# Two additions of the fast down projection moved between its items, and a longer planned wait ahead of the cross-chunk products of a recurrence

## The chip, the cores and the metric

The kernel runs on one core of one Trainium2 chip. The metric is the device time of one execution in microseconds (us), lower is better. A core has a matrix engine (PE, with its weight loads shown as a row of their own, PEld), a vector engine (DVE), a scalar engine (ACT), GpSimd (POOL) and SyncE (SP), which here only issues transfers. Each engine works through its own list of instructions in the order in which they were put there, and an instruction that waits for another engine holds up what stands behind it on its own.

## The reference

Two decoder layers on x of 512 tokens by 1024 channels, everything in float32. Each layer is a half-weighted SwiGLU block, a mixer and a second half-weighted SwiGLU block, each between two RMS norms:

```python
x = x + 0.5 * rms_norm(swiglu(rms_norm(x, g0), w_gate1, w_up1, w_down1), g1)      # 1024 -> 2816 -> 1024
h = rms_norm(x, g2); hq, hf, hi, hg, aq, ak, av, gate_a, gate_b = split(h @ w_in)
A = hgrn2_mixer(hq, hf, hi, hg, ...) @ w_branch_hgrn     # gated linear recurrence, 4 heads, 128 x 128
B = swa_sink_attention(aq, ak, av, sinks) @ w_branch_attn # window 128, 8 query and 2 key heads
x = x + rms_norm((sigmoid(gate_a) * A + sigmoid(gate_b) * B) @ w_out, g3)
x = x + 0.5 * rms_norm(swiglu(rms_norm(x, g4), w_gate2, w_up2, w_down2), g5)
```

In the recurrence a head's state is decayed by a gate per channel and token and takes up an outer product of key and value; the output is the state read with the query. The kernel computes it without a scan, as a causal 512 x 512 matrix of decayed scores times the values.

## The kernel before

**Products.** A float32 factor is carried as two parts, `hi` (rounded to the matrix engine's fast format) and `lo` (what is left), and a product is three matmuls, hi·hi, hi·lo and lo·hi (`mm3`). Every weight tile is loaded from DRAM by SP into one of four buffers `w32` (in the profile `w`), then ACT copies it into `whi` (L281 for the items of the fast down projection, L324 for the others) and DVE subtracts that from the tile into `wlo` (L286, L331). There are six `whi` and six `wlo` buffers, so the split runs a few items ahead of PE. A buffer of `w32` comes free, and the next load is issued, when the last split that reads it is done.

**The fast down projection.** Four times, once in each SwiGLU block, eight of the 22 blocks of rows of the down projection's weights (8 x 8 blocks of 128 x 128) are multiplied by a scheme of seven instead of eight products of quarters (`ORDER`: p1, p6, p2, p7, p5, p4, p3). Each product is 24 matmuls of 512 columns, from two items with q = 0 and 1, and `quarters` writes their order for PE. `quarter` prepares an item: p1, p2, p4 and p5 use a raw quarter of the weights, the others sums of quarters. With b12 and b22 loaded beside the raw tiles, p6 makes `t2` = b11 - b12 - b22 in a buffer of the tag `tt` (L267, L268). p7 adds b22 onto b12 (L276), which is its own weight, and also adds t2 onto the raw quarter b21 (L277), which only p4 reads. Each addition is two instructions of 128 x 512 per item. `pin` keeps the additions of these lines in the written order among themselves. On DVE there also stand the sums of the products' results: `add` (L789) forms u2 from product 6 and p1, u3 from product 7 and u2, and later two more from product 5. L789 reads PSUM and so waits for the product's matmuls, and the PSUM buffer of the product comes free when it is done.

The tag `tt` has two buffers. The tile `grow` (a row of gains, L664) is the next to take the older one, so its transfer, issued by SP, waits for the last reader of t2.

**The order of PE.** PE's order is written out while the program is built: the main line of the program issues projections and products, and after each it polls a planner (`Order`), which keeps a planned time `t` in ns and adds to it a price for every matmul. Work that depends on other engines is written as generators. Each yields a number of planned ns (the table `WAIT`), and its next piece is put into PE's order at the first poll at which that many planned ns have passed, with a pause of WAIT["rest"] between two pieces. For the other engines a scheduler chooses the order from the program's text and its own estimates, so that it moves when PE's order moves.

**The recurrence.** `recurrence_scores` handles two heads at a time, twice per layer. Its last steps are:

```python
yield WAIT["last"]            # then p1 = aux(): products of chunks 0,1 and 2,3 of both heads
...                           # L1047, L1048: eight scalings of the keys and queries, in place, on DVE; L1049 copies p1
yield WAIT["chunks"]
for h in hs:                  # the cross-chunk products of the two heads, one PSUM buffer each
    h.s2 = big(F32, [P, 2, 2 * P]); p2 = aux()
    for s in range(2):
        mm(p2[:, s * 256 : (s + 1) * 256], h.kz[:, s * P : (s + 1) * P], h.qa[:, 256:512], True, True)
    nc.scalar.copy(h.s2, p2...)   # L1057
```

PSUM buffers of the tag `aux` (three of them) serve these products, the scores of the attention (`attend`, two buffers at a time, read by DVE at L1157) and others in turn. A softmax block of the attention continues on ACT (L1174) and returns to DVE (L1178: `den`). The first pair of heads runs while PE computes the values of the recurrence from the tokens (`project_tok`, four `acc` buffers), beside the attention's first blocks; the second pair while PE computes the branches.

Of the kernel before, what the change touches and what calls it, by code (L numbers as in the profile page):

```python
# [11 lines left out]
ALU = mybir.AluOpType  # L12
# [18 lines left out]

WAIT = dict(
    first=0.0, spread=2300.0, squares=1700.0, lay=34500.0, laid=770.0, normed=7600.0, final=2600.0,
    head=2600.0, level=5000.0, last=3400.0, chunks=1270.0, blocks=350.0, norm=2370.0, gate=8000.0,
    values=1200.0, scores=2000.0, exp=9000.0, shares=4500.0, turn=1900.0, turned=3000.0, rest=1200.0, lent=4200.0, apart=4000.0, block=2000.0, pair=4000.0, att0=1260.0, att1=12300.0,
)
W32, WS, AHEAD, TAIL, PLAIN, FIRST, EARLY, LATE = 4, 6, 3, 4, 4, 7, 4, 8
# [8 lines left out]
def trunk(ctx: ExitStack, tc: tile.TileContext, xin, wall, gains, lbT, hgain, sinks, c_dist, c_mask, c_ident, out):  # L46
    nc = tc.nc
# [11 lines left out]
    def nm(s):  # L59
        seq[0] += 1  # L60
        return f"{s}_{seq[0]}"
# [83 lines left out]
    pin = tc.keep_in_program_order  # L145
# [10 lines left out]
    class Stream:  # L156
# [98 lines left out]
        def quarter(self, it):  # L255

            self.load(it.base + 4)
            q, h = it.q, (slice(0, S), slice(S, D))
            if it.kind in ("p1", "p2", "p5", "p4"):
                w = [self.raw[it.u][:, c] for c in h]  # L260
            elif it.kind == "p6":

                t = sb.tile([P, D], F32, tag="tt", name=nm("tt"), bufs=2)
                self.t2[q] = w = [t[:, c] for c in h]
                for c in range(2):
                    t1 = self.raw[it.u][:, h[c]]
                    pin(nc.vector.tensor_tensor(t1, t1, self.b12[q][c], op=ALU.subtract))  # L267
                    pin(nc.vector.tensor_tensor(w[c], t1, self.b22[q][c], op=ALU.subtract))  # L268
            elif it.kind == "p3":
                w = self.b22[q]  # L270
            elif it.kind == "p7":

                w = self.b12[q]
                for c in range(2):
                    b21 = self.raw[it.base + 2 + q][:, h[c]]
                    pin(nc.vector.tensor_tensor(w[c], w[c], self.b22[q][c], op=ALU.add))  # L276
                    pin(nc.vector.tensor_tensor(b21, b21, self.t2[q][c], op=ALU.add))  # L277
            it.hi = sb.tile([P, D], F32R, tag="whi", name=nm("whi"), bufs=WS)
            it.lo = sb.tile([P, D], F32R, tag="wlo", name=nm("wlo"), bufs=WS)
            for c in range(2):  # L280
                nc.scalar.copy(it.hi[:, h[c]], w[c])  # L281
                if it.kind in DMAS:
                    nc.scalar.mul(it.lo[:, h[c]], w[c], -1.0)
                    nc.gpsimd.dma_start(it.lo[:, h[c]].bitcast(F32), w[c], accum_op=ALU.add)
                else:
                    nc.vector.tensor_tensor(it.lo[:, h[c]], w[c], it.hi[:, h[c]].bitcast(F32), op=ALU.subtract)  # L286
            self.done += 1
            self.flight += 1
            if it.kind in ("p5", "p4"):
                self.raw.pop(it.u)  # L290
                self.freed += 1
                self.load(self.freed + W32)
# [1158 lines left out]
```

## Time and profile before

| | |
|---|---|
| median of 3 runs | 2108.14 us (2106.92 to 2108.67) |
| the profiled execution | 2106.95 us, span in the trace 2104.9 us, so 2.05 us lie around the span |
| its place among the runs | 1.19 us below the median |
| granted clock of PE | 0.999 |
| busy PE, PEld, DVE, ACT, POOL | 2093.2, 1875.4, 1549.3, 1122.6, 154.2 us |

The page gives each engine's busy time and share of the span. The view of waits sums, by the line that waited and the line that ended the wait, how long an engine stood idle. The timeline lists instructions by their start, equal neighbours merged: start, duration, engine, line, operation, tiles, shapes, count, and in brackets the idle time ahead of it and what ended it. Matmuls overlap, so the spacing of their starts says how fast they go, and not their durations.

### The profile page before, as it was taken

The page shows a single profiled execution, that of the slowest core. Times are in us where ns is not written, and L with a number is a line of the kernel's source. Part 1 is how long each engine was busy: PE and PEld are TensorE (multiplying, and loading weights), DVE is VectorE, ACT ScalarE, POOL GpSimd, SP SyncE. Part 2 cuts the span into 40 slices and gives each one's busy share as a digit, 9 for nine tenths or more (in the row PEclk, how much of TensorE's full clock was granted, in tenths as well). Part 3 has the DMA queues.
Part 4 walks back from the last instruction along what each step waited for, and adds up shares of the span by engine and source line. Part 5 has one row for each costly group of instructions (what it writes and reads, how often), then busy time and mean ns, then how long its engine had stood idle before and what let it go on. Part 6 is the DMA issues. An engine that isn't in the chain of part 4 may idle for free.

```text
span 2104.9 us, 35214 instructions
## 1 busy us (share of the span) xinstructions
PE 2093.2 (99%) x13549; PEld 1875.4 (89%) x13549; DVE 1549.3 (74%) x2705; ACT 1122.6 (53%) x1899; POOL 154.2 (7%) x188
## 2 busy tenths in 40 slices
PE   9999999999999999999999999999999999999998
PEld 7899988877888999998899998898778989999987
DVE  5877886766776777789587778767686758777884
ACT  6555554446454555556355556444654545555562
POOL 0011000000000011110001110000000000111000
PEclk9999999999999999999999999999999999999999
DMA  8677653312236357774447775632122563677651
GB/s 247 152 181 184 176 164 127 111 61 70 72 101 201 127 123 181 181 194 128 151 114 176 183 181 149 190 121 91 51 81 61 136 190 106 158 182 181 182 164 47
DMA packets 148071, 298.35 MB, mean 142 GB/s; under 512 B 16992, under 2 KB 74816, under 8 KB 147904
## 3 DMA queue, kind: packets, MB, share of 16 engines
q1 hardware_dynamic: 122416, 228.16, 33.1%
q0 software_dynamic: 25344, 67.91, 18.7%
q8 instruction: 106, 1.74, 0.3%
q14 instruction: 61, 0.50, 0.1%
q10 hardware_dynamic: 144, 0.05, 0.0%
HBM read 213.43 MB, written 14.73 MB: 108 GB/s over the span
## 4 chain that ended last, share of the span: by engine, by line
PE 80%; DVE 9%; ACT 6%; issue 2%; DMA 2%; SPq 0%; ACTq 0%; DVEq 0%
PE acc L115 59%; PE aux L115 19%; ACT whi L324 2%; DMA w<-wall 2%; DVE s L401 1%; PE aux L125 1%; DVE wlo L331 1%; DVE wlo L286 1%; ACT s L400 1%; ACT m L894 1%; ACT wlo L328 1%; PE acc L125 1%; DVE tt L318 1%; DVE tt L311 1%; DVE tt L268 0%
## 5 line engine op out<-in xcount | busy, mean ns | idle before, releaser
L115 PE MATMUL acc<-s,whi 128*128 128x256 f32 (+1 forms) x4952 | 1059.4, 311 | 0.9 <-ACT whi L324 0.7
L115 PEld LDWEIGHTS acc<-s,whi 128*128 128x128 f32 x4952 | 808.0, 191 | 51.8 <-issue 3.2
L115 PE MATMUL acc<-s,wlo 128*128 128x256 f32 (+1 forms) x2476 | 766.6, 310 | 0.1
L115 PEld LDWEIGHTS acc<-s,wlo 128*128 128x128 f32 x2476 | 472.6, 191 | 25.2 <-DVE wlo L331 0.4
L324 ACT CAST whi<-w 128x1024 fp32r<-128x1024 f32 (+1 forms) x341 | 317.0, 948 | 259.2 <-PE acc L115 99.9
L115 PE MATMUL acc<-whi,s 128*128 128x512 f32 x1264 | 414.0, 393 | 0.0
L324 ACT CAST whi<-tt 128x1024 fp32r<-128x1024 f32 x154 | 161.4, 1048 | 326.6 <-DVE tt L318 182.8
L331 DVE TENSOR_TENSOR wlo<-w,whi 128x1024 fp32r<-128x1024 f32 (+1 forms) x181 | 218.1, 1215 | 156.5 <-ACT whi L324 149.4
L115 PEld LDWEIGHTS acc<-whi,s 128*128 128x128 f32 x1264 | 237.1, 188 | 54.9 <-ACT whi L324 1.6
L331 DVE TENSOR_TENSOR wlo<-tt,whi 128x1024 fp32r<-128x1024 f32 x154 | 188.0, 1221 | 97.4 <-ACT whi L324 97.3
L115 PE MATMUL acc<-wlo,s 128*128 128x512 f32 x632 | 246.9, 391 | 1.0 <-DVE wlo L286 1.0
L115 PE MATMUL aux<-s,whi 128*128 128x256 f32 (+1 forms) x1248 | 230.5, 285 | 0.0
L329 POOL DMA_DIRECT2D wlo<-w x160 | 137.8, 863 | 1259.6 <-ACT wlo L328 732.2
L115 PE MATMUL aux<-whi,s 128*128 128x512 f32 x592 | 196.8, 390 | 0.0
L115 PEld LDWEIGHTS aux<-s,whi 128*128 128x128 f32 x1248 | 195.2, 192 | 1.1 <-issue 0.5
L115 PE MATMUL aux<-s,wlo 128*128 128x256 f32 (+1 forms) x624 | 177.6, 285 | 0.0
L115 PEld LDWEIGHTS acc<-wlo,s 128*128 128x128 f32 x632 | 118.7, 188 | 25.6 <-DVE wlo L286 2.4
L115 PEld LDWEIGHTS aux<-whi,s 128*128 128x128 f32 x592 | 111.1, 188 | 22.9
L328 ACT ACTIVATE wlo<-w 128x1024 fp32r<-128x1024 f32 (+1 forms) x160 | 129.8, 844 | 0.0
L400 ACT CAST s<-s 128x512 fp32r<-128x512 f32 (+1 forms) x164 | 88.6, 580 | 70.7 <-DVE s L459 66.6
L115 PEld LDWEIGHTS aux<-s,wlo 128*128 128x128 f32 x624 | 119.8, 192 | 0.4
L115 PE MATMUL aux<-wlo,s 128*128 128x512 f32 x296 | 115.2, 389 | 0.0
(186 smaller groups left out, 2127.6 us busy)
## 6 DMA issues: line engine op xcount, KB each, us to landing
w<-wall SPq DMA_DIRECT2D x267, 512.0 KB, 3.7
wlo<-w POOLq DMA_DIRECT2D x83, 512.0 KB, 5.5
w<-wall SPq DMA_DIRECT2D x288, 128.0 KB, 3.2
wlo<-w POOLq DMA_DIRECT2D x77, 256.0 KB, 3.3
x_d<-s SPq DMA_DIRECT2D x48, 256.0 KB, 2.1
s<-x_d SPq DMA_DIRECT2D x48, 256.0 KB, 5.3
w<-wall SPq DMA_DIRECT2D x34, 256.0 KB, 3.0
s<-wall SPq DMA_DIRECT2D x64, 128.0 KB, 3.6
```

Of the source, the lines that this page charges most:

```text
L115: nc.tensor.matmul(o, lhsT, rhs, start=start, stop=stop)
L125: nc.tensor.transpose(o, src, ident)
L286: nc.vector.tensor_tensor(it.lo[:, h[c]], w[c], it.hi[:, h[c]].bitcast(F32), op=ALU.subtract)
L311: pin(nc.vector.tensor_tensor(self.t13[:, h[0]], w[:, h[0]], v[:, h[0]], op=ALU.add))
L318: pin(nc.vector.tensor_tensor(t[:, h[1]], t[:, h[0]], w[:, h[1]], op=ALU.add))
L324: i = nc.scalar.copy(it.hi[:, c], w[:, c])
L328: nc.scalar.mul(it.lo[:, c], w[:, c], -1.0)
L329: nc.gpsimd.dma_start(it.lo[:, c].bitcast(F32), w[:, c], accum_op=ALU.add)
L331: nc.vector.tensor_tensor(it.lo[:, c], w[:, c], it.hi[:, c].bitcast(F32), op=ALU.subtract)
L400: nc.scalar.copy(hi, src)
L401: nc.vector.tensor_tensor(lo, src, hi.bitcast(F32), op=ALU.subtract)
L894: nc.scalar.activation(out=m[:, 0:2, :], in_=m[:, 0:2, :], func=AF.Silu)
```

## The change

Two edits. The two additions of t2 onto b21 leave item p7 and stand at the head of item p4 with the same q. The planned wait `chunks`, between the products of neighbouring chunks and the cross-chunk products, goes from 1270 to 2600 planned ns. The number of instructions is the same on every engine.

```diff
-    head=2600.0, level=5000.0, last=3400.0, chunks=1270.0, blocks=350.0, norm=2370.0, gate=8000.0,
+    head=2600.0, level=5000.0, last=3400.0, chunks=2600.0, blocks=350.0, norm=2370.0, gate=8000.0,
...
             if it.kind in ("p1", "p2", "p5", "p4"):
                 w = [self.raw[it.u][:, c] for c in h]
+                if it.kind == "p4":
+                    for c in range(2):
+                        pin(nc.vector.tensor_tensor(w[c], w[c], self.t2[q][c], op=ALU.add))
...
                 w = self.b12[q]
                 for c in range(2):
-                    b21 = self.raw[it.base + 2 + q][:, h[c]]
                     pin(nc.vector.tensor_tensor(w[c], w[c], self.b22[q][c], op=ALU.add))
-                    pin(nc.vector.tensor_tensor(b21, b21, self.t2[q][c], op=ALU.add))
```

The changed lines shift the later lines of the file. Inside `quarter`, L276 of before is L278 now and the moved additions are L263; from L278 of before on a line is one higher (L286 is L287, L664 is L665, L789 is L790, L1057 is L1058, L1157 is L1158).

The first place is DVE in the first of the four fast down projections, where the items of p7 are made; w_489 and w_492 are the raw b21 of q = 0 and 1, s_2765 to s_2772 are b12, s_2777 to s_2784 b22, s_3131 and s_3132 the two halves of u2. Before:

```order
L276 TENSOR_TENSOR s_2765<-s_2765,s_2777 128x512
L277 TENSOR_TENSOR w_489_2817<-w_489_2817,tt_2996 128x512
L276 TENSOR_TENSOR s_2766<-s_2766,s_2778 128x512
L277 TENSOR_TENSOR w_489_2817<-w_489_2817,tt_2996 128x512
L286 TENSOR_TENSOR wlo_3166<-s_2765,whi_3165 128x512
L286 TENSOR_TENSOR wlo_3166<-s_2766,whi_3165 128x512
L276 TENSOR_TENSOR s_2771<-s_2771,s_2783 128x512
L277 TENSOR_TENSOR w_492_2840<-w_492_2840,tt_3044 128x512
L276 TENSOR_TENSOR s_2772<-s_2772,s_2784 128x512
L277 TENSOR_TENSOR w_492_2840<-w_492_2840,tt_3044 128x512
L286 TENSOR_TENSOR wlo_3179<-s_2771,whi_3178 128x512
L286 TENSOR_TENSOR wlo_3179<-s_2772,whi_3178 128x512
```

These twelve are followed by the two additions to u2 (L789). Now, from behind the first two additions of L278 on:

```order
L790 TENSOR_TENSOR s_3131<-aux_3159,s_3129 128x512
L287 TENSOR_TENSOR wlo_3164<-s_2765,whi_3163 128x512
L287 TENSOR_TENSOR wlo_3164<-s_2766,whi_3163 128x512
L278 TENSOR_TENSOR s_2771<-s_2771,s_2783 128x512
L278 TENSOR_TENSOR s_2772<-s_2772,s_2784 128x512
L790 TENSOR_TENSOR s_3132<-aux_3160,s_3130 128x512
L287 TENSOR_TENSOR wlo_3175<-s_2771,whi_3174 128x512
L287 TENSOR_TENSOR wlo_3175<-s_2772,whi_3174 128x512
L287 TENSOR_TENSOR wlo_3204<-w_467_2710,whi_3203 128x512 x2
L287 TENSOR_TENSOR wlo_3218<-w_478_2760,whi_3217 128x512 x2
L263 TENSOR_TENSOR w_489_2817<-w_489_2817,tt_2996 128x512 x2
L790 TENSOR_TENSOR s_3133<-acc_3249,s_3131 128x512
```

Both halves of u2 have moved ahead of p7's `wlo`, one to each item, the additions onto b21 stand behind p5's `wlo`, and the first half of u3 (s_3133, from product 7) now stands ahead of p4's `wlo`.

The second place is PE in the mixer of the first layer, at the first pair of heads; acc_4617 to acc_4620 are the values projected from the tokens, aux_4766 and aux_4771 (now aux_4804 and aux_4809) the cross-chunk products of the two heads, aux_4788 and aux_4789 (now aux_4775 and aux_4776) the first scores of the attention's next block. Before:

```order
L115 MATMUL acc_4620<-whi_4486,s_3867 128x512
L115 MATMUL acc_4620<-wlo_4487,s_3867 128x512
L115 MATMUL acc_4620<-whi_4486,s_3868 128x512
L115 MATMUL aux_4766<-s_4258,s_4220 128x256 x2
L115 MATMUL aux_4771<-s_4263,s_4230 128x256 x2
L115 MATMUL acc_4617<-whi_4486,s_3870 128x512
L115 MATMUL acc_4617<-wlo_4487,s_3870 128x512
L115 MATMUL acc_4617<-whi_4486,s_3871 128x512
L115 MATMUL acc_4618<-whi_4486,s_3870 128x512
L115 MATMUL acc_4618<-wlo_4487,s_3870 128x512
L115 MATMUL acc_4618<-whi_4486,s_3871 128x512
L115 MATMUL aux_4788<-s_4290,s_4378 128x256
```

Now, three matmuls of acc_4617 and the twelve of the scores stand ahead of these:

```order
L115 MATMUL aux_4776<-s_4290,s_4424 128x256
L115 MATMUL acc_4618<-whi_4486,s_3870 128x512
L115 MATMUL acc_4618<-wlo_4487,s_3870 128x512
L115 MATMUL acc_4618<-whi_4486,s_3871 128x512
L115 MATMUL acc_4619<-whi_4486,s_3870 128x512
L115 MATMUL acc_4619<-wlo_4487,s_3870 128x512
L115 MATMUL acc_4619<-whi_4486,s_3871 128x512
L115 MATMUL aux_4804<-s_4258,s_4220 128x256 x2
L115 MATMUL aux_4809<-s_4263,s_4230 128x256 x2
L115 MATMUL acc_4620<-whi_4486,s_3870 128x512
```

The cross-chunk products have moved behind nine matmuls of the values and the twelve of the first scores, so these scores now take their PSUM buffers first. DVE follows: the readings of these scores (L1157) now stand ahead of `den` (L1178), behind which they stood.

At the second pair of heads of a layer the cross-chunk products move behind nine matmuls of a branch, and the outputs of these two heads with them. On SP, in each fast down projection, the transfer of `grow` now stands behind the eight transfers of the next two weight tiles instead of ahead of them, and one of the later loads of x stands behind a weight load that it stood ahead of. The lists of the second layer change in the same places.

## The prediction

> **What bounds the kernel now.** I read the page's first part, then the waits of PE and of its weight loads, then the timelines where those waits lie.
>
> ```profile
> PE 2093.2 (99%) x13549; PEld 1875.4 (89%) x13549; DVE 1549.3 (74%) x2705; ACT 1122.6 (53%) x1899; POOL 154.2 (7%) x188
> ```
>
> PE works through nearly the whole span, so time can come only from short stalls of PE, and only those that the two edits touch. The waits of PE name the lines of both edits:
>
> ```profile
> PE acc L115 <- DVE wlo L286: 1.0, 4, 0.3
> PE aux L115 <- DVE s L1048: 0.9, 2, 0.5
> PE aux L115 <- ACT s L1057: 0.7, 2, 0.3
> ```
>
> L286 is the `wlo` of the fast down projections (four places, one in each), L1048 the last scalings ahead of the cross-chunk products, L1057 the copy that frees one of their PSUM buffers (two places each, one per layer). By this view 2.6 us are at stake. The same view of the weight loads names the same lines, with more time:
>
> ```profile
> PEld acc L115 <- DVE wlo L286: 2.4, 4, 0.6
> PEld aux L115 <- DVE s L1048: 1.8, 2, 0.9
> PEld aux L115 <- ACT s L1057: 1.1, 2, 0.5
> PEld acc L115 <- ACT whi L281: 0.9, 3, 0.4
> ```
>
> That is 6.2 us. Which of the two sums is time of PE is settled by the starts of matmuls, against the same stretch undisturbed.
>
> **Part 1, the additions of p7.** The first fast down projection on PE (the third row is the second item's second matmul):
>
> ```profile
> 268.37 0.39 PE L115 MATMUL aux<-whi,s 128*128 128x512 f32 x1
> ...
> 273.81 0.39 PE L115 MATMUL acc<-whi,s 128*128 128x512 f32 x1
> ...
> 282.84 0.50 PE L115 MATMUL acc<-wlo,s 128*128 128x512 f32 x1 [0.29 <-DVE wlo L286]
> ...
> 285.47 0.39 PE L115 MATMUL aux<-whi,s 128*128 128x512 f32 x1
> ...
> 2011.26 0.39 PE L115 MATMUL acc<-whi,s 128*128 128x512 f32 x1
> ...
> 2022.77 0.39 PE L115 MATMUL aux<-whi,s 128*128 128x512 f32 x1
> ```
>
> From 268.37 to 273.81 runs product 6, 24 matmuls in 5.44 us, 0.227 each. From 273.81 to 285.47 run products 2 and 7, 48 matmuls, in 11.66 us instead of 10.88: 0.78 us lost. In the last of the four places (2011.26 to 2022.77) the same 48 take 11.51: 0.63 lost. The two places between lose 0.77 and 0.49 by the same two starts. Together 2.67 us. DVE at the first place:
>
> ```profile
> 275.48 0.68 DVE L276 TENSOR_TENSOR s<-s,s 128x512 f32<-128x512 f32 x1
> 276.08 0.68 DVE L277 TENSOR_TENSOR w<-w,tt 128x512 f32<-128x512 f32 x1
> ...
> 281.50 1.28 DVE L286 TENSOR_TENSOR wlo<-s,whi 128x512 fp32r<-128x512 f32 x2
> 282.71 1.28 DVE L789 TENSOR_TENSOR s<-aux,s 128x512 f32<-128x512 f32 x2
> 283.91 4.89 DVE L286 TENSOR_TENSOR wlo<-w,whi 128x512 fp32r<-128x512 f32 x8
> 288.72 1.28 DVE L789 TENSOR_TENSOR s<-acc,s 128x512 f32<-128x512 f32 x2
> ```
>
> Every addition here takes 0.60 us from start to start, L789 with its PSUM source too. Before, twelve of them run without a gap from 275.48, and the last `wlo` of p7 ends at 281.50 + 1.28 = 282.78; PE starts the matmul on it at 282.84. Undisturbed, product 7 begins at 273.81 + 5.44 = 279.25, and that matmul is its fourteenth, due at 279.25 + 13 x 0.227 = 282.20. Now four additions leave this stretch and two of L789 enter it: ten instructions, the last ending at 275.48 + 9 x 0.603 + 0.68 = 281.59, that is 0.6 us before it is due. Its first item's `wlo` is the fifth instruction, done at 278.6 against 279.47. ACT gets the sums earlier too, so the `whi` stall (L281) goes with it. The two L789 read product 6, which PE leaves at 273.81, almost 3 us before DVE comes to the first at 276.7, so they add their length and no wait. At the other places I take the same cover. The gain lies between 0, if the two L789 wait after all, and 2.67; I take 2.67, since the nearest rows show margins everywhere.
>
> What became later: the additions onto b21, the second half of u2 and the `wlo` of p4. The `wlo` of p5 now ends at 281.59 + 4 x 0.60 = 284.0 (before 286.3), wanted from 284.69 (product 7's end, undisturbed) and, for its second item, 2.9 us later. Then two additions, half of u3 (it waits for product 7, about 284.9), two `wlo`: p4's first item is done at about 287.0, its second after five more at about 290.0, wanted at 290.1 and 293.1 (product 5 takes 5.44). p3's four follow until 292.5, wanted at 295.6. So what is late next is p4's second item, with 3 us to spare. The additions cost DVE nothing new: as many instructions as before, and at these places DVE is ahead of PE again. The PSUM buffers of products 6 and 7 come free by 280.3 and 289.1, before products 5 and 3 begin to write there (284.7, 295.6).
>
> On SP:
>
> ```profile
> 278.03 0.33 SPq L664 DMA_DIRECT2D grow<-rows_d  x1
> 285.27 22.20 SPq L241 DMA_DIRECT2D w<-wall  x40
> ```
>
> The weight loads begin when p5's first `wlo` frees its buffer, 285.27; now at about 282.8. The transfer of `grow` waits for the additions onto b21 (285.2) and stands behind these two tiles' loads; the tile loads behind it wait for p4's `wlo`, 287.0 and 290.0, against 287.5 and 288.7 before. Their items are wanted by PE after product 3, from 301 on. Cost nothing; if that cover went, it could cost at most the 1.3 us by which one buffer is freed later.
>
> **Part 2, the wait `chunks`.** The first pair of heads on PE, first layer; then the same pieces undisturbed (the scores at 442.82, the products of the second pair of heads at 569.40), then the scores in the second layer:
>
> ```profile
> 434.12 0.40 PE L115 MATMUL acc<-whi,s 128*128 128x512 f32 x1
> 434.99 1.99 PE L115 MATMUL aux<-s,s 128*128 128x256 f32 x8 [0.47 <-DVE s L1048]
> 436.63 0.58 PE L115 MATMUL acc<-whi,s 128*128 128x512 f32 x1
> ...
> 437.98 0.40 PE L115 MATMUL acc<-whi,s 128*128 128x512 f32 x1
> ...
> 439.25 0.97 PE L115 MATMUL aux<-s,s 64*128 64x256 f32 x9 [0.33 <-ACT s L1057]
> ...
> 440.15 0.50 PE L115 MATMUL acc<-whi,s 128*128 128x512 f32 x1
> ...
> 442.82 0.39 PE L115 MATMUL acc<-whi,s 128*128 128x512 f32 x1
> ...
> 444.05 0.50 PE L115 MATMUL acc<-whi,s 128*128 128x512 f32 x1
> ...
> 569.40 0.39 PE L115 MATMUL acc<-s,wlo 128*128 128x512 f32 x1
> ...
> 571.16 0.81 PE L115 MATMUL acc<-s,whi 128*128 128x512 f32 x2
> ...
> 1479.21 0.40 PE L115 MATMUL acc<-whi,s 128*128 128x512 f32 x1
> ...
> 1481.39 0.50 PE L115 MATMUL acc<-whi,s 128*128 128x512 f32 x1
> ```
>
> From the last matmul ahead of the cross-chunk products to the first behind: 436.63 - 434.12 = 2.51 us, against 571.16 - 569.40 = 1.76 at the second pair, where nothing is waited for: 0.75 lost. Over the scores behind them: 440.15 - 437.98 = 2.17 against 444.05 - 442.82 = 1.23: 0.94 lost; second layer 1481.39 - 1479.21 = 2.18, the same. The products there lose the same (the waits of L1048 count two equal places). Two layers: 2 x (0.75 + 0.94) = 3.38 us. DVE and ACT there:
>
> ```profile
> 435.43 0.28 DVE L1048 TENSOR_SCALAR s<-s,s 128x128 f32<-128x128 f32 x1
> ...
> 438.76 0.17 DVE L1178 TENSOR_TENSOR den<-den,es 128x8 f32<-128x8 f32 x1 [2.97 <-ACT s L1174]
> ...
> 440.21 1.07 DVE L1157 SCALAR_TENSOR_TENSOR s<-dist,aux 128x256 f32<-128x256 f32 x3
> ```
> ```profile
> 438.63 1.04 ACT L1057 COPY s<-aux 128x512 f32<-128x512 f32 x2
> ```
>
> Now PE goes on at 434.35 with three matmuls, does the scores (about 435.1 to 436.0), six matmuls more, and reaches the cross-chunk products at about 437.5, 1.8 us behind the last scaling (435.71): the first stall is gone. Their first buffer is that of the chunk products, copied long before. The second is one that these scores used; DVE reads the scores (0.35 us each) from about 436.1, in the 2.97 us in which it sat waiting for the softmax, so it is free by 437 and wanted at 438.4. The next scores, at about 441, want the other one of these (free by 438.3) and the buffer of the first cross-chunk product: ACT copies it when its exponentials end, 438.63 to 439.15. So the second stall goes too, and nothing is left within 1.3 us. The nearest rows bound this part by 0 (if a wait of the same size appears at the new place) and 3.38; I take 3.38, since each wait above has its end before its need.
>
> At the second pair of heads the products lost nothing and the later place (nine matmuls, 2.0 us) gains nothing. Their outputs come 2.0 us later:
>
> ```profile
> 591.29 0.60 PE L125 MATMUL aux<-ident,s 128*128 128x128 f32 x4
> ...
> 612.03 0.63 PE L115 MATMUL acc<-s,whi 128*128 128x512 f32 x2
> ```
>
> The last transposes start at 591.29, the first product that uses them at 612.03: 20 us of cover hide a shift of 2.
>
> **Sum.** 2.67 + 3.38 = 6.05 us less. The profiled execution of 2106.95 would take 2100.9; it stands 1.19 below the median of the runs, so the forecast is 2102.1 us, 0.29% less. What is won on PE should stay won: in the stretches behind these places DVE and ACT wait for PE.
>
> The page "Perfetto Trace Analysis" of the Trainium skill (Identifying the Most-Contended Engine) holds that the busy time of matmuls misleads, since they are pipelined, and has weight loads looked at instead. By the row of PE the sum would be 2.6, by that of the weight loads 6.2; the starts, 6.05, side with the rule.
>
> **The rivals.** Only part comes back. The idle column of PE says 2.6 us (2105.5); the same time results if the stalls in the mixer stay (2.67), and 2104.8 if only the fast down projections bring nothing (3.38). For it: a margin of only 0.6 us at product 7. Against: the starts, and the order on DVE, which holds no other work there.
>
> Slower: u2 holds up DVE. L789 stands now ahead of p7's `wlo`; were it to get its result only with product 2's end (279.25) instead of product 6's, DVE would pass it at 279.4, 2.7 us late, the last `wlo` would end at 284.3, and PE would stall 2.1 us instead of 0.67 on the mean: 1.4 us lost at each of four places, 5.7. With the mixer's 3.38 the time would be 2110.5, without it 2113.8. It decides from a wait of 0.6 us on, which gives the stall back, and of 1.3 on, which makes it longer. Against it: DVE reaches L789 almost 3 us after PE has left product 6.
>
> No effect: the planner's price is in planned ns, and PE, ahead by some us, may meet the next late partner and wait there: 2107 to 2109. For it: DVE is busy without a gap at the fast down projections. Against: it is PE's own results that start that work, so it comes earlier too.
>
> **How the numbers follow.** About 0.2%, 4.2 us, is what a measurement of this kernel can tell from no change. Both parts in full or nearly (2101 to 2103.7): 0.77, all faster. One part only, by the idle column or otherwise (2104.8 to 2105.5): 0.12, within. No effect: 0.05, within. Slower by u2, 2110.5 to 2113.8: 0.06, of which 0.01 within and 0.05 over the bound. Faster 0.77, same 0.18, slower 0.05. The range: low, 6.2 us by the weight loads and the 1.2 us by which the fastest run lies under the median, 2108.14 - 7.4 = 2100.7; high, 2105.7, the part alone that brings least. The cases outside it hold about 0.13.
>
> **What would show it.** Right: from the end of product 6 to the start of product 5 PE takes 10.9 us at all four places, the waits of PE no longer name L287 (L286 of before), L1049 and L1058, and DVE reads the scores ahead of `den`. Wrong: a wait of DVE at L790 with PE behind it, a wait of the second cross-chunk product on L1158, or a new PE wait further down of the size of the gain.

## The result, and the profile after

The changed kernel takes 2101.21 us (median of 7 runs, 2100.53 to 2102.46), the kernel before on the same chip 2108.56 (7 runs): a ratio of 0.9967, 95% interval 0.9955 to 0.9978. Measured again beside the experiments, it was 2100.96 against 2108.25, ratio 0.9967, 0.9956 to 0.9979. The profiled execution took 2100.66 us, 6.29 less than that of before, with a span of 2098.9.

The page of the changed kernel, busy time by engine:

```profile
PE 2090.3 (100%) x13549; PEld 1875.3 (89%) x13549; DVE 1550.5 (74%) x2705; ACT 1122.4 (53%) x1899; POOL 154.2 (7%) x188
```

All that PE waits for now, and what is left of one of the three lines in the view of the weight loads (total us, times, longest):

```profile
PE acc L125 <- DVE s L731: 2.9, 1, 2.9
PE aux L115 <- DVE eps_t L138: 1.1, 1, 1.1
PE acc L115 <- ACT whi L325: 0.3, 1, 0.3
```
```profile
PEld aux L115 <- DVE s L1049: 0.7, 2, 0.4
```

L287 (`wlo`), L1049 (the scalings) and L1058 (the copy) are gone from PE's waits; the first two rows are the kernel's end and its start. The timeline of PE, from the start of product 2 to that of product 5 at the first and the last fast down projection, with the fourteenth matmul of product 7 between:

```profile
274.04 0.39 PE L115 MATMUL acc<-whi,s 128*128 128x512 f32 x1
...
282.43 0.39 PE L115 MATMUL acc<-wlo,s 128*128 128x512 f32 x1
...
284.92 0.39 PE L115 MATMUL aux<-whi,s 128*128 128x512 f32 x1
...
2005.93 0.39 PE L115 MATMUL acc<-whi,s 128*128 128x512 f32 x1
...
2016.81 0.39 PE L115 MATMUL aux<-whi,s 128*128 128x512 f32 x1
```

10.88 us at both, and at the two between: 48 matmuls without a gap, where 11.66 and 11.51 stood. DVE at the first place:

```profile
275.72 1.29 DVE L278 TENSOR_TENSOR s<-s,s 128x512 f32<-128x512 f32 x2
276.93 0.68 DVE L790 TENSOR_TENSOR s<-aux,s 128x512 f32<-128x512 f32 x1
...
279.94 0.68 DVE L790 TENSOR_TENSOR s<-aux,s 128x512 f32<-128x512 f32 x1
280.54 1.30 DVE L287 TENSOR_TENSOR wlo<-s,whi 128x512 fp32r<-128x512 f32 x2
...
284.16 1.29 DVE L263 TENSOR_TENSOR w<-w,tt 128x512 f32<-128x512 f32 x2
```

Neither L790 has a wait ahead of it (no brackets). The last `wlo` of p7 ends at 280.54 + 1.30 = 281.84, and PE wants it at 282.43: 0.59 us of margin. At the other three places the margin is 0.59 to 0.70 us. SP behind it:

```profile
283.06 4.97 SPq L241 DMA_DIRECT2D w<-wall  x8
288.13 0.38 SPq L665 DMA_DIRECT2D grow<-rows_d  x1
288.61 11.36 SPq L241 DMA_DIRECT2D w<-wall  x16
```

PE, DVE and ACT in the mixer of the first layer (scores, cross-chunk products, next scores):

```profile
434.27 0.39 PE L115 MATMUL acc<-whi,s 128*128 128x512 f32 x1
434.59 0.98 PE L115 MATMUL aux<-s,s 64*128 64x256 f32 x12
435.49 0.50 PE L115 MATMUL acc<-whi,s 128*128 128x512 f32 x1
...
436.78 0.39 PE L115 MATMUL acc<-whi,s 128*128 128x512 f32 x1
437.00 1.89 PE L115 MATMUL aux<-s,s 128*128 128x256 f32 x8
438.54 0.58 PE L115 MATMUL acc<-whi,s 128*128 128x512 f32 x1
...
439.88 0.40 PE L115 MATMUL acc<-whi,s 128*128 128x512 f32 x1
...
441.11 0.50 PE L115 MATMUL acc<-whi,s 128*128 128x512 f32 x1
```
```profile
435.59 1.08 DVE L1158 SCALAR_TENSOR_TENSOR s<-dist,aux 128x256 f32<-128x256 f32 x3 [0.35 <-PE aux L115]
...
438.21 0.17 DVE L1179 TENSOR_TENSOR den<-den,es 128x8 f32<-128x8 f32 x1 [0.61 <-ACT s L1175]
```
```profile
438.08 0.57 ACT L1058 COPY s<-aux 128x512 f32<-128x512 f32 x1
```

The scores take 1.22 us and 1.23, the products 1.76, which are the undisturbed values. DVE reads the scores ahead of `den`, in time in which it waited before.

### The profile page after: what moved, and what is told of

Same layout as the page of the kernel before. It is cut to its first block, busy times and chain, and to the rows that moved or that the text cites. A ratio compares the mean times of both kernels' runs of the same rounds, so it can differ in the third digit from the quotient of the medians.

```text
span 2098.9 us, 35207 instructions
## 1 busy us (share of the span) xinstructions
PE 2090.3 (100%) x13549; PEld 1875.3 (89%) x13549; DVE 1550.5 (74%) x2705; ACT 1122.4 (53%) x1899; POOL 154.2 (7%) x188
## 3 DMA queue, kind: packets, MB, share of 16 engines
q8 instruction: 106, 1.74, 0.3%
## 4 chain that ended last, share of the span: by engine, by line
PE 88%; DMA 0%; DVE 0%; ACT 0%; SPq 0%; issue 0%; ACTq 0%
PE acc L115 64%; PE aux L115 22%; PE aux L125 1%; PE acc L125 1%; DMA wlo<-w 0%; DMA w<-wall 0%; SPq L241 0%; DVE s L402 0%; ACT whi L282 0%; DVE s L731 0%; ACT s L600 0%; DVE s L712 0%; DVE s L896 0%; DVE wlo L287 0%; ACT m L895 0%
```

## The experiments

All times below are medians, and each kernel is compared with runs of the kernel before on its own chip: 2108.56 us for the first row of the changed kernel, 2107.78 for the additions alone, the wait alone, half of the move and chunks at 1600, 2108.25 for the others. Beside the times, each profiled execution gives the length of fixed stretches of PE, from start to start of the same two matmuls. "Products 2+7" runs from product 2 to product 5 in the four fast down projections. "Mixer" runs from the matmul ahead of the first scores (422.57 in the trace of before) to product 2 of the next down projection, in layer 1 and 2. "Total" runs from the first product 2 to the last matmul and leaves out the kernel's first 274 us.

| kernel | median us | products 2+7 | mixer | total |
|---|---|---|---|---|
| before | 2107.78, 2108.25 (26, 24 runs) | 11.66 11.65 11.37 11.51 | 547.55 547.45 | 1826.65 |
| before, second trace | 2108.92 (one run) | 11.71 11.68 11.67 11.68 | 547.75 547.70 | 1828.22 |
| before, third trace | 2108.70 (one run) | 11.69 11.68 11.68 11.49 | 547.75 547.45 | 1828.00 |
| changed | 2101.21 | 10.88 10.88 10.88 10.88 | 545.81 545.80 | 1820.39 |
| changed, again | 2100.96 | 10.88 10.88 10.88 10.88 | 545.80 545.93 | 1820.58 |
| additions only | 2104.66 | 10.88 10.88 10.88 10.88 | 547.58 547.44 | 1824.14 |
| wait only | 2103.47 | 11.67 11.68 11.66 11.53 | 546.09 545.78 | 1823.75 |
| half of the move | 2101.67 | 10.88 10.88 10.88 10.88 | 545.78 545.78 | 1820.73 |
| chunks 1600 | 2102.82 | 10.88 10.88 10.88 10.88 | 546.80 546.79 | 1822.57 |
| chunks 5500 | 2101.96 | 10.88 10.88 10.88 10.88 | 546.33 545.83 | 1821.85 |
| one more per item | 2107.51 | 12.41 12.22 12.35 12.38 | 545.78 546.35 | 1826.71 |
| two more per item | 2113.15 | 13.94 13.71 13.79 13.83 | 545.78 545.81 | 1832.32 |

**The additions alone.** The changed kernel with the wait put back:

```diff
-    head=2600.0, level=5000.0, last=3400.0, chunks=2600.0, blocks=350.0, norm=2370.0, gate=8000.0,
+    head=2600.0, level=5000.0, last=3400.0, chunks=1270.0, blocks=350.0, norm=2370.0, gate=8000.0,
```

> The additions moved as in the change, the wait chunks left at 1270. By the prediction's terms 2.67 us go, all of them in products 2 and 7 of the four fast down projections, which take 10.88 us from product 6's end to product 5's start; the mixer keeps its stalls (products 2.51, scores 2.17). That is 2105.9 us against the 2108.56 of before. If the idle column of PE were the true size, 1.0 us would go (2107.5). If PE only met the next late partner sooner, nothing (2108.5). If this edit alone made the whole gain, 2101.5.

Measured: 2104.66 us against 2107.78, ratio 0.9986 (0.9977 to 0.9995). All four stretches are at 10.88, the mixer is as before (547.58 and 547.44), and the waits of PE name the mixer's two lines with the numbers that they had before, and `wlo` no more:

```profile
PE aux L115 <- DVE s L1049: 0.9, 2, 0.5
PE aux L115 <- ACT s L1058: 0.7, 2, 0.3
```

The total is 2.51 us below the first trace of before. So by these stretches this edit acts in the four places and not in the mixer, and what is won there is not given back. The medians fell by 3.12 us where 2.67 were expected; most of the difference goes to the size of the stalls, which lose 2.97 on the mean of the three traces of before below.

**The wait alone.** Before, with `chunks=2600.0` and nothing else.

> Only the wait chunks at 2600, the additions left in p7. By the prediction's terms 2 x (0.75 + 0.94) = 3.38 us go: the stretch around the cross-chunk products takes 1.76 us instead of 2.51 and the scores 1.23 instead of 2.17, in both layers; the fast down projections keep 11.66, 11.65, 11.37 and 11.51 for products 2 and 7. That is 2105.2 us. By the idle column of PE 1.6 us would go (2107.0); if the later products met another late buffer or the outputs came late, 0 or less (2108.5 and above).

Measured: 2103.47 us against 2107.78, ratio 0.9981 (0.9972 to 0.9990). The cross-chunk products of the first layer take 1.76 us, the scores ahead of them 1.22 and the scores behind them 1.23, as expected. The mixer takes 546.09 and 545.78, and products 2+7 keep their stall:

```profile
PE acc L115 <- DVE wlo L286: 1.2, 4, 0.3
```

The third place lost 0.78 us here (11.66) where the first trace of before had 0.49: the same code, another execution. By the stretches the two edits do not touch each other's places, and their gains add up: the medians fell by 4.31 us here and by 3.12 with the additions alone, 7.43 together, against 7.29 with both.

**Half of the move.** With the change's wait, and in `quarter`

```diff
                 if it.kind == "p4":
-                    for c in range(2):
-                        pin(nc.vector.tensor_tensor(w[c], w[c], self.t2[q][c], op=ALU.add))
+                    pin(nc.vector.tensor_tensor(w[1], w[1], self.t2[q][1], op=ALU.add))
...
                     pin(nc.vector.tensor_tensor(w[c], w[c], self.b22[q][c], op=ALU.add))
+                b21 = self.raw[it.base + 2 + q][:, h[0]]
+                pin(nc.vector.tensor_tensor(b21, b21, self.t2[q][0], op=ALU.add))
```

> The change with half of the move: of the two additions per item, the one on the first half of b21 goes back to p7, behind p7's own two additions. Here u2 stands behind p7's wlo again, so ten instructions of DVE run from the first L277 to p7's last wlo, as many as in the changed kernel with both halves of u2 among them. The prediction's count (0.60 us each, due 0.6 us after the tenth) gives the whole gain: 10.88 us for products 2 and 7 at each place and the time of the changed kernel, 2101.2. If each addition that is moved brought its own share, half of 2.67 would stay: products 2 and 7 about 11.2, 2102.5. If u2 ahead of p7's wlo had cost the changed kernel something, this one would be faster than it.

Measured: 2101.67 us, ratio 0.9970 (0.9959 to 0.9982), and 10.88 at all four places. The timeline of DVE at the first of them, where product 2 began at 273.31:

```profile
274.84 1.28 DVE L277 TENSOR_TENSOR s<-s,s 128x512 f32<-128x512 f32 x2
276.05 0.68 DVE L279 TENSOR_TENSOR w<-w,tt 128x512 f32<-128x512 f32 x1
...
279.06 0.68 DVE L279 TENSOR_TENSOR w<-w,tt 128x512 f32<-128x512 f32 x1
...
279.66 1.30 DVE L288 TENSOR_TENSOR wlo<-s,whi 128x512 fp32r<-128x512 f32 x2
280.88 1.28 DVE L791 TENSOR_TENSOR s<-aux,s 128x512 f32<-128x512 f32 x2
```

Two additions per place moved instead of four, u2 (L791) behind p7's `wlo` again, and nothing is lost: the last `wlo` ends at 280.96, and PE wants it at 273.31 + 8.39 = 281.70. What counts here is how many of these instructions of 0.60 us stand ahead of that `wlo`, ten as in the changed kernel, and not which: from the first of them to the end of the last it takes 280.96 - 274.84 = 6.12 us here and 281.84 - 275.72 = 6.12 there. So u2 ahead of that `wlo` costs its length and no more.

**One and two more instructions per item.** The changed kernel, with this in p7 (in the first for c = 1 only, in the second for both halves):

```diff
                     pin(nc.vector.tensor_tensor(w[c], w[c], self.b22[q][c], op=ALU.add))
+                    pin(nc.vector.tensor_tensor(w[c], w[c], w[c], op=ALU.max))
```

> The changed kernel with one more addition-sized instruction of DVE per item of p7 (the larger of a half and itself, in place, which leaves the values as they are). With it, thirteen instructions of DVE run from the first L278 to p7's last wlo (ten in the changed kernel, twelve in the kernel before): one of p5's wlo has come in between as well. By the prediction's count the last wlo ends at 275.48 + 12 x 0.603 + 0.68 = 283.4, 1.2 us after it is due: products 2 and 7 take 12.1 us at each place, 4 x 1.2 = 4.8 us more than in the changed kernel, 2106.0. If PE were not bound by this chain (the gain came from elsewhere, or a slack swallows it), 10.9 and 2101.2.

> The same with two more instructions per item of p7, one on each half: fifteen from the first L278 to p7's last wlo. It ends at 275.48 + 14 x 0.603 + 0.68 = 284.6, 2.4 us late: products 2 and 7 take 13.3 us, 4 x 2.4 = 9.6 us more than in the changed kernel, 2110.8, slower than before the change. If a delay ahead of p7's wlo is worth less than its length (as a slack further on would have it), less: half of it gives 2106.

Measured: 2107.51 us (10 runs) and 2113.15 (8 runs) against 2108.25 for the kernel before and 2100.96 for the changed one, ratios to before 0.9998 (0.9989 to 1.0008) and 1.0026 (1.0016 to 1.0036). With one more the gain is gone, with two more the kernel is slower than before. The stretches grew by 1.34 to 1.53 us and by 2.83 to 3.06, where 1.2 and 2.4 were expected. The first of these kernels, DVE and then PE at the first place, where product 2 began at 274.03:

```profile
283.08 0.69 DVE L288 TENSOR_TENSOR wlo<-s,whi 128x512 fp32r<-128x512 f32 x1
```
```profile
283.82 0.50 PE L115 MATMUL acc<-wlo,s 128*128 128x512 f32 x1 [0.43 <-DVE wlo L288]
284.15 0.62 PE L115 MATMUL acc<-whi,s 128*128 128x512 f32 x2
```

The `wlo` ends at 283.77, 9.74 behind product 2's start, where the count gave 283.4 - 273.81 = 9.59. PE starts 0.05 later, which is 1.40 after its due time of 274.03 + 8.39, and the next matmul follows at 0.33 instead of 0.227. So the count was right on DVE to 0.15 us, and a stall costs PE some 0.15 us more than the lateness. With two more per item the count was further off. There the last `wlo` ends 11.22 behind product 2's start (274.26 to 285.48), where the count gave 284.6 - 273.81 = 10.79; why DVE was 0.43 us slower is not shown. PE starts 0.05 later again, and 13.94 - 10.88 = 3.06 are lost at the first place, of it 1.25 already at the first item.

These kernels also say which view sizes a stall. Two more per item lost 55.27 - 43.52 = 11.75 us at the four places by the starts. The waits of PE, and then of its weight loads, say:

```profile
PE acc L115 <- ACT whi L284: 4.5, 8, 0.8
...
PE acc L115 <- DVE wlo L289: 2.6, 8, 0.4
```
```profile
PEld acc L115 <- ACT whi L284: 7.9, 8, 1.2
PEld acc L115 <- DVE wlo L289: 5.1, 8, 0.7
```

7.1 and 13.0 us. With one more, the starts say 49.36 - 43.52 = 5.84, and the two views:

```profile
PE acc L115 <- DVE wlo L288: 2.2, 7, 0.4
```
```profile
PEld acc L115 <- DVE wlo L288: 5.2, 8, 0.7
...
PEld acc L115 <- ACT whi L283: 1.8, 4, 0.5
```

2.2 and 7.0. In these two kernels the idle time in the view of PE counts four to six tenths of the stalls, that of the weight loads a tenth to a fifth too much.

**An earlier and a later place for the cross-chunk products.** The changed kernel with `chunks=1600.0`, and with `chunks=5500.0`.

> The changed kernel with chunks at 1600 instead of 2600: the cross-chunk products stand behind nine matmuls of the values (six before) and still ahead of the attention's scores. Two separate stalls: PE reaches the products 0.68 us later than before (three matmuls of 0.227), so the first stall falls from 0.75 to about 0.07, while the scores still wait for the copy that ACT makes at about 438.6 behind its exponentials, 0.94 to 1.0 us. Both layers: 2 x (0.07 + 0.97) = 2.1 us stay, 2103.3. If the second stall is only the first one handed on, both go: 2101.2 to 2101.4. If the products' later place alone brings nothing, 3.4 stay: 2104.6.

> The changed kernel with chunks at 5500: the first pair's cross-chunk products go behind one more block of the attention's scores and twelve more matmuls of the values, 4 us later than in the changed kernel, and the second pair's some 3 us later. If only the place behind the first scores counts, and the later outputs stay covered (20 us at the second pair), nothing changes: 1.76 us for the products, 1.23 for both scores, 2101.2 us. If the products' buffers are then those of the second scores and these are read late, a stall of up to 0.9 per layer comes back: 2103. If the outputs come late, a new wait of PE behind them of some us.

With 1600: 2102.82 us, ratio 0.9975 (0.9965 to 0.9984). The timeline of PE in the first layer:

```profile
434.19 0.39 PE L115 MATMUL acc<-whi,s 128*128 128x512 f32 x1
434.42 1.94 PE L115 MATMUL aux<-s,s 128*128 128x256 f32 x8
436.00 0.58 PE L115 MATMUL acc<-whi,s 128*128 128x512 f32 x1
...
437.34 0.39 PE L115 MATMUL acc<-whi,s 128*128 128x512 f32 x1
...
438.62 0.97 PE L115 MATMUL aux<-s,s 64*128 64x256 f32 x9 [0.35 <-ACT s L1058]
439.52 0.51 PE L115 MATMUL acc<-whi,s 128*128 128x512 f32 x1
```

The products take 1.81, the scores 2.18 with the copy of L1058 named. Three matmuls more ahead of the products take 0.70 of the first stall's 0.75, and the second stays whole at 0.95. So there are two separate stalls: the first is one of distance from the scalings; the second stays while the products stand ahead of the scores, and is gone in every kernel here in which the scores stand ahead of the products. The mixer stretches, 546.80 and 546.79, are 0.99 above the changed kernel's, as 0.05 + 0.95 says.

With 5500 the products begin 3.9 us later than in the changed kernel and take 1.76, both scores 1.23, so the stalls stay away. The time, 2101.96 us (8 runs, ratio 0.9973, 0.9962 to 0.9983), is 1.0 above that of the changed kernel measured beside it, and the total is 1.3 to 1.5 longer. None of it lies at the moved products: layer 2's mixer is unchanged (545.83), layer 1's longer by 0.52 through a delay at 946, in front of the next down projection, and another 0.67 fall between the second and the third fast down projection, where the third trace of before lost 0.95 against the first. Both delays lie at the same point of the program, some 96 matmuls ahead of product 2. There six matmuls take 1.36 us from start to start when nothing is late, and 1.54 to 2.23 at one or more of the four places in eleven of the twelve traces of this document, 2.20 in that third trace of before. So these delays are of a kind that comes and goes without any edit; that the later place has no part in them is not shown.

**The two kernels once more.** The changed kernel and the kernel before, each without an edit; of before two executions were profiled.

> The changed kernel once more, on the same chip as the experiments: the prediction's terms give 6.05 us less than the kernel before here; 7.35, the difference of the medians in the first measurement, would say that 1.3 us come from something that the terms leave out.

> The kernel before once more, for a second profiled execution of it. The medians fell by 7.3 us, the stalls in the first pair of traces by 6.05. If the rest lies in what varies between executions (the first profiled execution of before was 1.2 us faster than its median), this trace has the same four stalls of 0.5 to 0.8 us in products 2 and 7, the same 0.75 and 0.94 in the mixer, and a longer span by stalls elsewhere or by a larger stall at one of the places. If the terms left out a steady stall, it appears in this trace and the first at the same place and in none of the changed kernel.

> A third profiled execution of the kernel before, to the same end: the stretches that the terms rest on repeat to 0.1 us in the mixer and to 0.3 us in products 2 and 7; the others differ between executions of the same kernel as much as between the two kernels.

The new traces of before have the same stalls in the mixer (2.50 or 2.51 us over the products and 2.17 to 2.19 over the scores in all three traces and both layers), and larger ones in products 2+7. The third place in the second trace of before:

```profile
1316.11 0.39 PE L115 MATMUL acc<-whi,s 128*128 128x512 f32 x1
...
1327.78 0.39 PE L115 MATMUL aux<-whi,s 128*128 128x512 f32 x1
```

That is 11.67, where the prediction had 11.37. Over the four places the three traces lose 2.67, 3.22 and 3.02 us. The totals are 1826.65, 1828.22 and 1828.00, the changed kernel's 1820.39 and 1820.58: on the means 1827.62 - 1820.49 = 7.1 us. The rest that differs between the traces of before lies where short waits come and go from execution to execution, as in the third trace:

```profile
1294.56 0.50 PE L115 MATMUL acc<-whi,s 128*128 128x512 f32 x1 [0.21 <-ACT s L400]
```

So the trace on which the prediction was built was one of the quicker executions of that kernel. The mixer stretches repeat to 0.3 us over its three traces, the loss in products 2+7 to 0.6.

## Why the prediction was right

**Part 1** was forecast at 2.67 us, the whole of the stalls in the first trace of before, and they went whole: four stretches at 10.88. Its details held: the last `wlo` 0.59 us ahead of its need (0.6 forecast), u2 without a wait, p5's loads on SP from 283.06 (282.8 forecast, by a clock 0.23 earlier). The additions alone show the term by itself. Half of the move shows that two of the four additions would have been enough. The added instructions show that past the margin the stall rises with each one, by 0.6 us and more. The term was still somewhat small, since it was read from one execution: the mean loss over three traces of before is 2.97.

**Part 2** was forecast at 3.38 us. The mixer stretches fell by 547.55 - 545.81 = 1.74 and 547.45 - 545.80 = 1.65, together 3.39. That the first stall goes by distance and the second by the order of scores and products was in the working, and chunks at 1600 separates the two as expected. The wait alone gained more by its medians, 4.31 us; 0.3 of that lie outside the span (told below).

**The edits at nothing.** The transfer of `grow` came later than worked out, 288.13 instead of behind 285.2 and two loads at once, because SP takes 4.97 us to issue those eight; the loads behind it go out at 288.61 instead of 287.0. No wait of PE followed. The later outputs of the second pair of heads cost nothing that shows: the mixer stretch, which holds them, fell by the two stalls in full.

**The sum** of 6.05 gave 2100.9 for the profiled execution, which took 2100.66. The step to the median was the weaker one. It kept the distance of 1.19 us that the first profiled execution of before had from its median, and so gave 2102.1; the changed kernel's profiled execution stood only 0.55 below its median. The forecast lay 0.9 above the median measured: the sum was 1.3 us short, and 0.4 of that was offset by chance, since seven runs of the kernel before had a median of 2108.56 where the first three had 2108.14. The medians differ by 7.3 us. Of that, 7.1 stand in the mean totals above, about 3.0 of them in products 2+7 and 3.5 in the mixers (the mean of three traces of before against two of the changed kernel), and some 0.6 in stretches that neither edit touches and that scatter as much between executions of one kernel; 0.33 more lie outside the span, told below, and 0.2 less come from the first 274 us, which were that much longer in the two traces of the changed kernel. The time was inside the range, but its upper end was not what its reason gives: the part alone that brings least makes 2108.14 - 2.67 = 2105.5, and not 2105.7.

**The rivals.** "Only part comes back" with the idle column of PE as the size (1.0 and 1.6 us) fell by the two edits taken alone: 2.51 and 2.90 in the total, 3.1 and 4.3 in the medians. "Slower by u2" needed L790 to wait for product 2; it shows no wait, and with u2 behind p7's `wlo` again the time and the stretches are the same. Its price was right in kind. With one more per item the last `wlo` of the first place comes 1.35 us after its due time, products 2+7 take longer there than before the change (12.41 against 11.66), and with the mixer's gain the kernel is where it was; with two more it comes 2.83 late, and the kernel is slower than before. "No effect" fell with the totals. The Trainium skill's page "Perfetto Trace Analysis" (Identifying the Most-Contended Engine) prefers the busy share of weight loads to that of matmuls for judging how close a kernel is to roofline. The size of a stall is another question, and there the traces here point the same way: the view of the weight loads is the nearer one, 13.0 against 7.1 where the starts say 11.75, and 7.0 against 2.2 where they say 5.84.

## What to carry to other kernels

When the bounding engine is 99% busy, size a stall by the starts of its instructions over a fixed stretch against the same stretch undisturbed: here the waits of PE showed 2.6 us of what was 6 to 7, and stretches compared across kernels showed where each edit acts to a few tenths of a microsecond, while single executions of one kernel scatter by 2 to 3. Before an instruction is moved out of a feeding engine's list, count the instructions ahead of the one that is waited for and multiply by their spacing: the gain stops once the last one meets its due time (two of the four moved additions were enough), and the same count gives, 10 to 30% too low here, the price of putting some too many there. Read such stalls from two or three executions; one trace was off by 0.3 to 0.6 us in 3.

## What the runs showed of the hardware that was not expected

The time around the span (the time of an execution less its span in the trace) isn't a constant of the program's frame. In the 50 runs of the kernel before that stand beside these experiments it was 2.04 to 2.15 us, with the additions alone 2.06 to 2.12, but 1.72 to 1.85 in the 50 runs of the changed kernel, the wait alone, half of the move, chunks at 1600 and one more per item. With chunks at 5500 and two more per item it took values from 1.76 to 2.15. So the 0.3 us came with the longer wait and not with the moved additions, but not in all executions of every kernel that has that wait. It was in no term, the trace shows nothing of it, and its cause stays open.

A stall of PE on a late `wlo` cost more than the lateness: 0.05 to 0.06 us from the end of the `wlo` to the start of its matmul, and 0.33 to 0.34 us instead of 0.227 to the start behind it, at p7's last `wlo` in all four places of the kernel before and of the kernels with one and two more per item.
